# Shifting the weight tiles of 512-column products by eight offsets in turn

## The chip, the cores and the metric

The kernel runs on one core of a Trainium2 chip. The metric is the device time of one execution in microseconds (us), on the slowest core, which here is the only one. Engines are named as in the profile: PE is TensorE's matmul, PEld is TensorE's weight load, DVE is VectorE, ACT is ScalarE, POOL is GpSimd, and SP issues most of the DMAs.

## What is computed

The reference is a two-layer decoder trunk on 512 tokens of width 1024. Cut to its skeleton:

```python
for layer in range(2):
    h = rms_norm(x, ln_mix[layer])
    mem_k, mem_v = split(mem_n @ w_mem_kv[layer])            # 256 memory tokens
    if layer == 0:
        mix_out, mem_q = gated_deltanet_mixer(h, ...)         # h @ w_in, conv, chunked delta rule
    else:
        proj = h @ swa_w_q                                    # sliding-window attention, 12 heads
        mix_out, mem_q = sliding_window_attention(...), ...
    x = x + concat(mix_out, memory_attention(mem_q, mem_k, mem_v)) @ w_out[layer]
    x = x + swiglu(rms_norm(x, ln_ffn[layer]), w_gate_up[layer], w_down[layer])   # d_ff = 2816
    if layer == 0:
        shared_k, shared_v = split(rms_norm(x, ln_kv) @ w_kv)
return rms_norm(x, ln_final)
```

Everything is float32. The bulk of the arithmetic is the products of the activations with the weight matrices.

## The kernel before

Activations are kept transposed: features on the 128 partitions, the 512 tokens along the free dimension. A product of a weight tile with the activations is done in three fp32r matmuls per 128 input features: the weight and the activation are each split into a high and a low part (`whi`, `wlo` and `h`, `l`), and `mm3` issues high by high, high by low, and low by high, one after the other. In each of them the weight slice (128 partitions by 128 columns, 512 bytes per partition) is loaded into TensorE by a weight load of its own, and the activation tile is the moving operand that streams past it. The order of instructions on every engine is the order in which the code is written; PE loads the next matmul's weights while a matmul streams.

The products fall into two kinds.

- **Wide products**, 512 columns (all tokens at once), made by `project`, `row`, the loop over `down` and a few direct calls. Their weights come from `weight`, which loads a raw tile of up to 1024 columns by DMA, and splits it: ACT copies (and rounds) it into `whi`, DVE subtracts and writes `wlo` (`split`). The two tiles come from `parts`, a pool of three buffers for each name, 1088 words (of 4 bytes) a partition. By the code there are 26 wide products of 24 matmuls in the first mixer, 10 in the second, 16 for the output matrices, 8 for the first gate columns, and 16 (less two at the end) for the down projection, which takes 12 and then 10 input tiles in two weight tiles: one call of `weight` for 6 input tiles, one for the other 6 or 4. That is 624 + 240 + 384 + 192 + 528 + 468 = 2436 matmuls of 512 columns, in 120 calls of `weight`. Ten further calls of `weight` serve 252 matmuls of 256 columns (the memory's keys and values at the start, where for the values the weight tile is the moving operand, and one product at the end).
- **The ring**, 256 columns (`quarters`, 3360 matmuls): most of the gate and up columns of the feed-forward part, multiplied by a scheme that needs seven half-size products. Their weights lie in the same pool, at a fixed shift of `SHIFT` = 52 words (208 bytes) from the start of a buffer.

Where an operand lies matters here. Every buffer starts at a multiple of 256 bytes, and so do all activation tiles and all their halves; a slice of 128 columns moves a weight by 512 bytes. So in a wide product of before, the weights lie 0 bytes modulo 256 from their moving operand. In the ring the moving operand lies 48 bytes after the weights, modulo 256 (256 - 208). At the very end, the last product (tile name `T`) has weights from a pool of its own, again at 0, with 256 columns.

Of the kernel before, what the change touches and what calls it, by code (L numbers as in the profile page):

```python
# [27 lines left out]
FT = DFF // P  # L28
EPS = 1e-6
LINE = 64  # L30
SHIFT, SPARE = 52, 64
NEG = -1e30
BASE = 32
NB = P // BASE
# [54 lines left out]
class Builder:  # L89
    def __init__(self, tc, a):  # L90
        self.tc, self.nc, self.a = tc, tc.nc, a
        self.n = 0
        self.table, self.table_ins, self.table_users = None, None, []


# [97 lines left out]
    def weight(self, src, eng=None, raw=None, parts=1, pool=None, tags=("whi", "wlo"), bufs=3):  # L193

        raw = self.load(src) if raw is None else raw
        n = raw.shape[1]
        if pool is None:
            hi, lo = (x[:, :n] for x in self.parts())
        else:
            hi, lo = (self.t(pool, [P, D], F32R, t, bufs)[:, :n] for t in tags)  # L200
        for i in range(parts):
            s = slice(i * n // parts, (i + 1) * n // parts)
            self.split(raw[:, s], hi[:, s], lo[:, s], eng or self.weng)
        return hi, lo
# [1086 lines left out]
```

## Time and profile before

| | |
|---|---|
| median of 2 runs | 1148.13 us (1147.78 to 1148.49) |
| the profiled execution's own time | 1148.39 us |
| its span in the trace | 1146.6 us |
| PE / PEld busy | 98% / 86% of the span |
| DVE / ACT / POOL busy | 73% / 55% / 7% |
| granted TensorE clock | 0.998 |

Times in the trace count from the start of the span. What lies around the span is 1.8 us (1148.39 - 1146.6). A matmul's duration in the trace runs from its start to the modelled arrival of its last result, so durations of neighbours overlap; the pace of a stretch of matmuls is the time from the first start to the last, divided by their number. The view that follows the chain of work back from the last instruction, printed in order of time, gives such stretches with their length and count.

### The profile page before, as it was taken

The page shows a single profiled execution, that of the slowest core. Times are in us where ns is not written, and L with a number is a line of the kernel's source. Part 1 is how long each engine was busy: PE and PEld are TensorE (multiplying, and loading weights), DVE is VectorE, ACT ScalarE, POOL GpSimd, SP SyncE. Part 2 cuts the span into 40 slices and gives each one's busy share as a digit, 9 for nine tenths or more (in the row PEclk, how much of TensorE's full clock was granted, in tenths as well). Part 3 has the DMA queues.
Part 4 walks back from the last instruction along what each step waited for, and adds up shares of the span by engine and source line. Part 5 has one row for each costly group of instructions (what it writes and reads, how often), then busy time and mean ns, then how long its engine had stood idle before and what let it go on. Part 6 is the DMA issues. An engine that isn't in the chain of part 4 may idle for free.

```text
span 1146.6 us, 19668 instructions
## 1 busy us (share of the span) xinstructions
PE 1127.0 (98%) x7476; PEld 990.7 (86%) x7476; DVE 841.2 (73%) x1587; ACT 631.5 (55%) x1271; POOL 86.0 (7%) x97
## 2 busy tenths in 40 slices
PE   7999999999999999999999999999999999999996
PEld 5888887887899998899998777778999988999986
DVE  5764887766789987489866777759699843898754
ACT  7579572366556652256654556765566522566533
POOL 0220000000101100011100000010011100111000
PEclk9999999999999999999999999999999999999999
DMA  8333342325657744567723411144477733577232
GB/s 312 124 116 108 123 107 97 99 86 166 175 142 190 189 125 125 151 151 182 184 74 101 138 56 56 56 111 129 105 191 188 187 108 106 141 191 185 70 96 93
DMA packets 73972, 152.83 MB, mean 133 GB/s; under 512 B 17757, under 2 KB 18421, under 8 KB 73877
## 3 DMA queue, kind: packets, MB, share of 16 engines
q1 hardware_dynamic: 62356, 130.59, 36.8%
q0 software_dynamic: 11520, 20.98, 11.6%
q8 instruction: 59, 0.97, 0.4%
q14 instruction: 37, 0.30, 0.1%
HBM read 144.58 MB, written 6.96 MB: 132 GB/s over the span
## 4 chain that ended last, share of the span: by engine, by line
PE 89%; DVE 5%; ACT 4%; DMA 1%; issue 1%; SPq 0%; DVEq 0%; ACTq 0%
PE pj L154 44%; PE g L154 38%; PE sc L154 6%; ACT sm L142 2%; DVE wlo L161 1%; PE g L158 1%; DMA wraw<-in_wmk 1%; DVE q L161 0%; DVE sm L784 0%; PE qk L154 0%; ACT sm L148 0%; DVE l L164 0%; ACT whi L148 0%; ACT pf L148 0%; DVE l L161 0%
## 5 line engine op out<-in xcount | busy, mean ns | idle before, releaser
L148 ACT ACTIVATE whi<-wraw 128x512 fp32r<-128x512 f32 (+2 forms) x331 | 243.9, 746 | 244.9 <-PE pj L154 151.8
L161 DVE TENSOR_TENSOR wlo<-wraw,whi 128x512 fp32r<-128x512 f32 (+2 forms) x331 | 274.8, 840 | 102.6 <-ACT whi L148 96.8
L154 PE MATMUL pj<-h,whi 128*128 128x512 f32 (+1 forms) x676 | 267.4, 397 | 0.2 <-ACT h L148 0.2
L154 PE MATMUL pj<-l,whi 128*128 128x512 f32 (+1 forms) x676 | 264.2, 391 | 0.6 <-DVE l L164 0.4
L154 PE MATMUL pj<-h,wlo 128*128 128x512 f32 (+1 forms) x676 | 264.0, 390 | 0.0
L154 PE MATMUL g<-T,whi 128*128 128x256 f32 x1280 | 228.1, 278 | 0.2
L154 PEld LDWEIGHTS g<-T,whi 128*128 128x128 f32 x1280 | 194.7, 188 | 1.8 <-DVE fu L164 1.8
L154 PE MATMUL g<-T,wlo 128*128 128x256 f32 x640 | 177.8, 278 | 0.0
L154 PEld LDWEIGHTS pj<-h,whi 128*128 128x128 f32 x676 | 126.8, 188 | 31.2 <-issue 5.8
L154 PEld LDWEIGHTS pj<-l,whi 128*128 128x128 f32 x676 | 127.1, 188 | 26.8 <-issue 1.1
L154 PEld LDWEIGHTS pj<-h,wlo 128*128 128x128 f32 x676 | 127.0, 188 | 25.7 <-issue 0.3
L154 PE MATMUL g<-h,whi 128*128 128x256 f32 (+1 forms) x508 | 144.5, 285 | 0.0
L154 PE MATMUL g<-h,wlo 128*128 128x256 f32 (+1 forms) x508 | 144.3, 284 | 0.0
L154 PE MATMUL g<-l,whi 128*128 128x256 f32 (+1 forms) x508 | 144.2, 284 | 0.0
L154 PEld LDWEIGHTS g<-T,wlo 128*128 128x128 f32 x640 | 120.1, 188 | 0.0
L154 PEld LDWEIGHTS g<-h,whi 128*128 128x128 f32 x508 | 95.3, 188 | 1.5 <-issue 0.3
L154 PEld LDWEIGHTS g<-l,whi 128*128 128x128 f32 x508 | 95.3, 188 | 1.2
L154 PEld LDWEIGHTS g<-h,wlo 128*128 128x128 f32 x508 | 95.3, 188 | 1.1
L1025 POOL DMA_DIRECT2D ws<-in_wgu x40 | 35.4, 885 | 693.6 <-DMA ws<-in_wgu 274.9
L148 ACT ACTIVATE whi<-ws 128x512 fp32r<-128x512 f32 x80 | 50.5, 631 | 49.0 <-PE g L154 40.2
L161 DVE TENSOR_TENSOR fu<-pj,rstd 128x512 f32<-128x512 f32 (+1 forms) x34 | 22.4, 660 | 54.5 <-PE pj L154 54.4
L161 DVE TENSOR_TENSOR wlo<-ws,whi 128x512 fp32r<-128x512 f32 x80 | 54.9, 686 | 6.4 <-ACT whi L148 6.3
(355 smaller groups left out, 1617.9 us busy)
## 6 DMA issues: line engine op xcount, KB each, us to landing
wraw<-in_wgu SPq DMA_DIRECT2D x48, 512.0 KB, 4.3
ws<-in_wgu SPq DMA_DIRECT2D x80, 256.0 KB, 3.5
ws<-in_wgu POOLq DMA_DIRECT2D x80, 256.0 KB, 4.8
wraw<-in_wdn SPq DMA_DIRECT2D x48, 384.0 KB, 3.1
wraw<-in_win SPq DMA_DIRECT2D x26, 512.0 KB, 3.6
wraw<-in_wgu SPq DMA_DIRECT2D x40, 256.0 KB, 4.2
wraw<-in_wout SPq DMA_DIRECT2D x16, 512.0 KB, 3.6
wraw<-in_wdn SPq DMA_DIRECT2D x16, 256.0 KB, 2.7
```

Of the source, the lines that this page charges most:

```text
L142: ins = self.nc.scalar.activation(out, in_, func, **kw).ins
L148: self.copied = self.nc.scalar.activation(out, in_, AF.Copy, **kw).ins
L154: return self.nc.tensor.matmul(out, lhsT, rhs, start=start, stop=stop, skip_group_check=more).ins
L158: return self.nc.tensor.transpose(out, in_, self.ident[:k, :k]).ins
L161: return eng.tensor_tensor(out=out, in0=a, in1=b, op=op).ins
L1025: nc.gpsimd.dma_start(s1, a22, accum_op=ALU.add)
```

## The change

`weight` no longer puts the parts at the start of their buffers. A counter goes round a list of eight shifts, in words, and each call takes the next one for both parts. Measured from the weights up to the moving operand, modulo 256 bytes, the eight distances are 4, 252, 12, 244, 20, 236, 56 and 72 bytes. The buffers stay as large as they were; the ring and the pool of the last product are not touched.

```diff
-SHIFT, SPARE = 52, 64
+SHIFT, WIDE, SPARE = 52, (63, 1, 61, 3, 59, 5, 50, 46), 64
...
         self.n = 0
+        self.wide = 0
...
         if pool is None:
-            hi, lo = (x[:, :n] for x in self.parts())
+            o = WIDE[self.wide % len(WIDE)]
+            self.wide += 1
+            hi, lo = (x[:, o:o + n] for x in self.parts())
```

No instruction is added, removed or moved: on every engine the same instructions stand in the same order with the same waits, with other start addresses in `whi` and `wlo` (in the line numbers of helpers, one to three more). Of the 2436 wide matmuls, 318 get a distance of 4, 300 of 252, 318 of 12, 300 of 244, 312 of 20, 288 of 236, 312 of 56 and 288 of 72.

## The prediction

> **What bounds the kernel now.** I read the page's busy times first, then the chain of work that ended last, then the same chain in order of time, and last the groups of instructions by shape.
>
> ```profile
> PE 1127.0 (98%) x7476; PEld 990.7 (86%) x7476; DVE 841.2 (73%) x1587; ACT 631.5 (55%) x1271; POOL 86.0 (7%) x97
> PE 89%; DVE 5%; ACT 4%; DMA 1%; issue 1%; SPq 0%; DVEq 0%; ACTq 0%
> PE pj L154 44%; PE g L154 38%; PE sc L154 6%; ACT sm L142 2%; DVE wlo L161 1%; PE g L158 1%; DMA wraw<-in_wmk 1%; DVE q L161 0%; DVE sm L784 0%; PE qk L154 0%; ACT sm L148 0%; DVE l L164 0%; ACT whi L148 0%; ACT pf L148 0%; DVE l L161 0%
> ```
>
> The kernel is bound by PE: 89% of the chain. The wide products write banks called pj for the most part, and those alone are 44% of 1146.6 us, some 504 us; the ring writes g. So what counts is the pace at which PE takes one matmul after the other. The chain in order of time shows that pace, in stretches:
>
> ```profile
> 162.43 2.08 PE pj L154 x9
> 166.66 2.08 PE pj L154 x9
> ...
> 290.61 5.44 PE g L154 x24
> 296.05 16.32 PE pj L154 x72
> ...
> 329.60 96.60 PE g L154 x828
> 428.98 64.20 PE pj L154 x283
> 493.18 93.82 PE g L154 x805
> 592.45 46.72 PE pj L154 x206
> ...
> 679.30 2.09 PE pj L154 x9
> ...
> 1130.73 5.88 PE pj L154 x49
> ```
>
> Columns are the start, the length in us and the number of matmuls. Four paces come out of it.
>
> - Wide, in a long stretch: 16.32 / 72 = 226.7 ns a matmul of 512 columns; 64.20 / 283 = 226.9 and 46.72 / 206 = 226.8 are the same with a few slower ones at the start.
> - Wide, in the first nine matmuls after a stop: 2.08 / 9 = 231.1 ns, and 2.09 / 9 = 232.2 ns. So PE has a settled pace, and it takes some ten matmuls to reach it.
> - The ring, 256 columns at a distance of 48 bytes: 96.60 / 828 = 116.7 ns.
> - The last product, 256 columns: 5.88 / 49 = 120.0 ns, in a part where, by the addresses, the weights lie at 0 bytes.
>
> Between 120.0 (256 columns) and 226.7 (512 columns), both at 0, lie 106.7 ns for 256 columns. So 512 columns by themselves are 213.3 ns, and each matmul has some 13.3 ns beyond its columns, whatever its length; in the ring it is 116.7 - 106.7 = 10.0 ns. That remainder is all that the change can reach. The groups by shape bear the 256-column pair out, in durations that hold the pipeline too:
>
> ```profile
> L154 PE MATMUL g<-T,whi 128*128 128x256 f32 x1280 | 228.1, 278 | 0.2
> L154 PE MATMUL pj<-l,T 128*128 128x256 f32 x16 | 4.5, 283 | 0.0
> L154 PE MATMUL pj<-h,whi 128*128 128x512 f32 x660 | 262.9, 399 | 0.2 <-ACT h L148 0.2
> L154 PE MATMUL pj<-l,whi 128*128 128x512 f32 x660 | 259.7, 394 | 0.6 <-DVE l L164 0.4 <-DVE l L161 0.2
> ```
>
> 278 ns at 48 bytes against 283 at 0: the address of the weights is worth something on this chip.
>
> **The change part by part.** Nothing is added, removed or moved in any queue, so there is no term for instructions. Three things can cost or gain.
>
> *First, the settled pace at eight other distances.* The trace has no wide product at any distance but 0, so I bound it by the nearest rows. On the good side stands the ring: 120.0 - 116.7 = 3.3 ns a matmul. If all 2436 wide matmuls gained that, it would be 8.0 us; the whole remainder of 13.3 ns, which no row shows removed, would be 32.4 us. On the bad side stands the pace after a stop: 231.1 - 226.7 = 4.4 ns, 10.7 us over 2436, and 232.2 - 226.7 = 5.5 ns, 13.4 us. The two nearest rows lie at almost equal distance from today's pace. With eight distances, none of which is a multiple of 16 bytes as 48 is, some should land on each side; I take the middle of -3.3 and +4.4, which is +0.5 ns, 1.3 us. I keep -3.3 and +5.5 as ends.
>
> The Trainium skill, page "TensorE: Matmul & The Clock Gate", section "Step-by-step: what each phase is for", says that TensorE has two independent read ports into SBUF, so that loading the next weights takes nothing from the running matmul. By that rule the distance would be worth nothing, and this first term would be 0. The 278 against 283 ns, and 116.7 against 120.0, speak against it, if the two cases differ by nothing but the address; it is the ground for one of the rivals below.
>
> *Second, settling anew.* Now a whole stretch of wide products has one distance, and PE settles once: 283 matmuls at 226.9. After the change the distance is another one at each call of the weight function, after 12 to 24 matmuls. If what settles is the relation between the stream of weights and the moving stream, each call starts it afresh. A settling costs nine matmuls of 4.4 ns, 0.04 us. Of the 120 calls I take 40 to stand behind a stop already (the first mixer's scan, the attention of layer 1, where the chain has stretches of 9 matmuls as shown), a choice from the shape of the chain, which leaves 80: 80 x 0.04 = 3.2 us. Below, the bound is 0 (PE keeps its pace across the change of distance, as it does now when it goes on to another buffer); above, 120 x 0.05 = 6.0 us.
>
> *Third, the writers.* ACT writes the high part and DVE the low part at addresses that are 4, 8 or 12 bytes off a multiple of 16. Writes like that stand in the trace already, in the convolution, whose taps write from 4, 8 and 12 bytes on:
>
> ```profile
> L164 DVE SCALAR_TENSOR_TENSOR l<-x,gains,h 128x512 fp32r<-128x512 f32 x32 | 23.5, 749 | 1.5 <-ACT h L148 1.5
> L164 DVE SCALAR_TENSOR_TENSOR qv<-pj,gains,qv 128x511 f32<-128x511 f32 x11 | 8.2, 745 | 4.7 <-ACT qv L148 4.6
> L164 DVE SCALAR_TENSOR_TENSOR qv<-pj,gains,qv 128x509 f32<-128x509 f32 x11 | 8.2, 741 | 0.1
> 447.00:494.00 47.00, 47.00 (x213) 39.08 (x212) 24.33 (x37) 12.16 (x17) 4.37 (x5) 1.00 0.55 143
> ```
>
> 745 and 741 ns against 749 at an aligned address: for DVE it costs nothing. For ACT there is no such row with 512 elements. The last line is the busy time by engine over 47 us of down projection (PE, PEld, DVE, ACT, POOL): PE is busy all the time, DVE for 24.33 us and ACT for 12.16, so ACT could take half as long again and PE would still hide it. I cost the writers at 0. If that cover were gone (the scan of layer 0 and the attention, where ACT and DVE stand in the chain), one tenth more on the 4% of ACT in the chain would be some 4 to 5 us at the very most.
>
> The 252 matmuls of 256 columns that also move would gain 0.8 us at the ring's 3.3 ns, or lose as much; I leave them at 0. Of the wide matmuls' 552 us (2436 x 226.7) 504 us are in the pj part of the chain alone, so what PE gains or loses there reaches the end almost in full. A faster PE would not run into late weights in the down projection, by the same line of busy times.
>
> The sum against the profiled execution's own 1148.4 us: +1.3 for the paces, +3.2 for settling, 0 for the writers: 1152.9 us. The median of the runs shown lies 0.3 us lower than that execution, so 1152.6 us, and I put 1152.5.
>
> **The rivals.**
>
> *A gain like the ring's.* Every distance other than 0 frees the moving stream of what the ring has lost, and PE keeps its pace from product to product: -8.0 us, 1140.1 from the median. For it speaks the only measured pair of distances; against it, that this pair has 256 columns, where the weight load covers the whole matmul, and a distance of a multiple of 16 bytes, and that in a wide product half the stream runs without a weight load beside it. If the distances are better than 48, a pace of 221 ns would give -13.9 us, 1134.
>
> *PE never settles (slower).* The place is the down projection and the long stretches of 226.7 ns: there the settled pace belongs to the distance 0, and at odd distances PE stays at what it has after a stop. The price is 4.4 ns on 2436 matmuls, 10.7 us, 1158.8 us; with 5.5 ns, 1161.5 us. It decides from the point where more than half the calls do not come down to 226.7 within their 12 to 24 matmuls. For it speaks that the pace after a stop is 231 to 232 in stretches of different products; against it, that the ring, at a distance other than 0, runs at a pace just as steady, over 828 matmuls.
>
> *Nothing happens.* The difference of 3.3 ns is due to something other than the distance (the ring's matmuls write other banks), and the settled pace is kept throughout: 1148.1 us, within 1 us. That is also where the rule of two read ports would lead.
>
> **How the numbers follow.** My forecast, a mix of paces with new settling, has a chance of 0.44, and spans 1146 to 1157 us, leaving out the near-zero case. The gain has 0.31 (1132 to 1146), the unsettled PE 0.18 (1157 to 1165), nothing 0.07. A range that leaves out no more than one in ten at each end reaches to 1137 below (the gain with its better half only partly in) and to 1161 above (the unsettled pace at 4.4 ns, with a little more). Two per cent, about what a measurement of this kernel can tell from no change, is 23 us, or 9.4 ns for each wide matmul. For a gain of that size PE would have to lose almost its whole remainder, 13.3 ns down to 3.9; for such a loss it would have to run at 236 ns, more than any stretch shown. So faster by over 2% has 0.03, slower by over 2% 0.03, and within 2% 0.94.
>
> **What would show it.** In the profile of the changed kernel, the chain in order of time around the down projections has to be read for its pace: 226.9 ns over 283 matmuls becomes 228 to 229 by my forecast, 223 by the gain, 231 by the unsettled PE. Since the distances go in turn, the starts of the matmuls inside one product show the pace of that distance: I expect some of the eight under 226.7 and some over, and the first ten of a product slower than the rest. The group of 660 matmuls named pj<-l,whi should go from 394 ns to 395 to 397; DVE's and ACT's splits should keep their durations; the ring should stay at 116.7 and the last product's T matmuls at 283 ns. I am wrong if a product at one distance shows no slow start (no settling), or if all eight distances lie on one side of 226.7.

## The result, and the profile after

The changed kernel takes 1157.82 us (median of 2 runs, 1157.55 to 1158.1) against 1148.13: a ratio of 1.0085, 95% interval 1.006 to 1.0109. It is slower by 9.7 us: inside the wide range of 1137 to 1161 us and within 2%, but more than twice the loss of the forecast (4.4 us), and just outside the 1146 to 1157 us that belonged to the forecast's own mechanism. The span of the profiled execution went from 1146.6 to 1156.3 us at the same granted clock, 0.998.

The page's busy times and its chain by engine:

```profile
span 1156.3 us, 19668 instructions
PE 1137.0 (98%) x7476; PEld 991.0 (86%) x7476; DVE 840.4 (73%) x1587; ACT 631.5 (55%) x1271; POOL 86.0 (7%) x97
PE 90%; DVE 4%; ACT 3%; DMA 1%; issue 1%; SPq 0%; DVEq 0%; ACTq 0%
```

The number of instructions is the same, the writers (DVE, ACT) and the weight loads (PEld) are as busy as before, and PE is busy for 10.0 us more. The chain in order of time (start, length, number of matmuls; lines left out are marked) tells where:

```profile
298.33 16.76 PE pj L155 x72
...
332.71 96.60 PE g L155 x828
432.11 65.78 PE pj L155 x283
...
597.16 47.78 PE pj L155 x206
...
925.05 65.77 PE pj L155 x283
...
1140.47 5.85 PE pj L155 x49
```

The stretch of 72 wide matmuls, 226.7 ns each before, is at 16.76 / 72 = 232.8; the 283 of each down projection went from 226.9 to 232.4 ns, the 206 from 226.8 to 231.9. The ring, in g, stands at 96.60 / 828 = 116.7 ns as it did. So the loss sits in the pace of the wide products, all over the program.

For the pace at each distance I took the starts of successive wide matmuls from the trace, and the distance of each from the built program's addresses (stops, gaps of 260 ns and more, left out). The mean is 232.2 ns, 227.5 before, a difference of 4.7. Of the 2436 wide matmuls 2242 follow another one in this way; 4.7 x 2242 = 10.5 us, which is near the 10.0 us that PE is busier and the 9.7 us of the kernel. By distance, from the tenth matmul of a product on (a product here is a run of matmuls into one bank at one distance):

| distance, bytes | 4 | 252 | 12 | 244 | 20 | 236 | 56 | 72 | 0 (before) |
|---|---|---|---|---|---|---|---|---|---|
| mean pace, ns | 232.9 | 232.5 | 233.0 | 232.9 | 231.6 | 233.3 | 230.6 | 231.9 | 226.7 |

All eight means lie on the bad side. None shows a slow start and a fall: at 236 bytes the first matmuls take 232.3, 230.9, 232.2, 233.1, and then it is 233.3 to the end. The starts fall into short patterns that repeat, such as 231 229 232 235 at 20 bytes.

One correction to the description above: the buffers do not start at multiples of 256 bytes but 192 bytes above one, weights and activations alike. The distances are as stated.

### The profile page after: what moved, and what is told of

It is laid out like the page before. It is cut to its first block, busy times and chain, and to the rows that moved or that the text cites. A ratio compares the mean times of both kernels' runs of the same rounds, so it can differ in the third digit from the quotient of the medians.

```text
span 1156.3 us, 19668 instructions
## 1 busy us (share of the span) xinstructions
PE 1137.0 (98%) x7476; PEld 991.0 (86%) x7476; DVE 840.4 (73%) x1587; ACT 631.5 (55%) x1271; POOL 86.0 (7%) x97
## 4 chain that ended last, share of the span: by engine, by line
PE 90%; DVE 4%; ACT 3%; DMA 1%; issue 1%; SPq 0%; DVEq 0%; ACTq 0%
PE pj L155 45%; PE g L155 38%; PE sc L155 6%; ACT sm L143 2%; DVE wlo L162 1%; PE g L159 1%; DMA wraw<-in_wmk 1%; DVE q L162 0%; DVE sm L787 0%; DVE l L165 0%; PE qk L155 0%; ACT sm L149 0%; DMA kn<-q 0%; ACT whi L149 0%; ACT pf L149 0%
```

## The experiments

Eleven kernels were run. All but one differ from the changed kernel in the list of shifts alone (a shift of s words is a distance of 256 - 4 s bytes).

**One distance or eight.** Is it the distances, or going from one to the next at each call?

```diff
-SHIFT, WIDE, SPARE = 52, (63, 1, 61, 3, 59, 5, 50, 46), 64
+SHIFT, WIDE, SPARE = 52, (61,), 64        # distance 12
+SHIFT, WIDE, SPARE = 52, (52,), 64        # distance 48, the other kernel
```

> All wide products at one distance, 12 bytes, instead of eight in turn. Theory A (each distance has a settled pace of its own; what the changed kernel showed at 12 bytes was 233.3 ns from the second half of a product on): every long stretch of wide products settles at 233.3 ns, the down projections' stretch of 283 matmuls takes 66.0 us, and the time is 1148.1 + 2436 x (233.3 - 226.7) x 0.85 = some 1161 to 1163 us, slower than the eight in turn. Theory B (a distance as such costs nothing, but changing it from call to call keeps PE from settling): 226.7 ns, and 1148 to 1150 us.

> All wide products at the ring's distance, 48 bytes. Theory A with a gain like the ring's (3.3 ns a matmul): a pace of 223.4 ns, and 1140 us. Theory A, if what helps 256 columns does not help 512 (a matmul stream of twice the length, with a weight load beside half of it only): a pace between 228 and 232 ns, 1151 to 1158 us. Theory B: 226.7 ns and 1148 us. The prediction's first term rested on the first of these.

Distance 12 took 1159.62 us (ratio 1.0098, 1.0082 to 1.0113), 48 took 1156.36 us (1.0073, 1.0056 to 1.009), against 1148.01 of the kernel before, run beside them. The chain of distance 12, then of 48:

```profile
432.39 66.02 PE pj L155 x283
```

```profile
430.52 65.62 PE pj L155 x283
```

66.02 / 283 = 233.3 ns at 12 bytes and 65.62 / 283 = 231.9 at 48. The pace at 12 is that of theory A, the time a little under its 1161 to 1163 us. So a single distance, kept throughout, is as slow as eight in turn: going from one to the next is not what costs. And the ring's distance, which beside 256 columns leaves 10.0 ns beyond the columns, leaves 231.9 - 213.3 = 18.6 ns beside 512. The gain of the ring does not carry over; it changes sign.

**Which distances are good.** Three lists of eight, one run each:

```diff
+... WIDE ... (60, 56, 52, 48, 44, 40, 36, 32)     # 16, 32, ... 128
+... WIDE ... (28, 24, 20, 16, 12, 8, 4, 0)        # 144, 160, ... 240, 0
+... WIDE ... (62, 58, 54, 42, 38, 34, 30, 26)     # 8, 24, 40, 88, ... 152
```

> The eight distances 16, 32, 48, 64, 80, 96, 112 and 128 bytes in turn, so that one profile shows the pace of each. Theory A: each has its own pace; multiples of 64 may behave as 0 does (226.7), the others 228 to 233; time 1150 to 1158 us. Theory C (only distances that are no multiple of 16 cost, since their weights begin inside a line of 16 bytes): all eight run at 226.7 or less, 1140 to 1149 us. Theory B: all slow, 231 to 233, since they change from call to call.

> The eight distances 144, 160, 176, 192, 208, 224, 240 and 256 (that is, 0) bytes in turn. Theory A: the products at 0 run at 226.7 ns among the others, the rest at 228 to 233, and the paces mirror those of 112 down to 16 if only the size of the distance counts; 1150 to 1157 us. Theory C: all at 226.7 or less. Theory B: the products at 0 are as slow as the rest, 231 or more.

> The eight distances 8, 24, 40, 88, 104, 120, 136 and 152 bytes in turn, to see whether any beats the 226.7 ns of 0. Theory A with a narrow best place from 0 to 16 bytes: 8 between 226.7 and 230, 24 near 228 to 231, the others 230 to 234; 1155 to 1158 us. If the good place is only at exact multiples of 16 next to 0: 8 and 24 at 231 to 233 as well.

They took 1155.14, 1157.41 and 1156.53 us. The pace from the tenth matmul on, in ns, worked out as above:

| | | | | | | | |
|---|---|---|---|---|---|---|---|
| 16: 227.6 | 32: 233.4 | 48: 231.8 | 64: 228.6 | 80: 230.0 | 96: 233.6 | 112: 233.2 | 128: 233.1 |
| 144: 233.3 | 160: 234.1 | 176: 231.9 | 192: 233.4 | 208: 233.4 | 224: 233.3 | 240: 233.4 | 0: 226.7 |
| 8: 233.3 | 24: 231.2 | 40: 232.3 | 88: 233.3 | 104: 231.3 | 120: 233.3 | 136: 226.7 | 152: 233.3 |

Theory C (only weights off a line of 16 bytes are slow) falls: 32, 96, 144 and 160 are as slow as any, and 48 was slow alone. It is no mirror image either (16 is good, 240 is not), and no narrow place around 0 (8 is bad, 136 is good). The products at 0 stand at 226.7 among seven bad ones, which they reach in some ten matmuls (232, 232, 230, 230, 229, 228, 228, 227, 228, 227). That is the settling of the prediction: the first ten average some 229.1, about 24 ns a call beyond 226.7. These are paces in turn; what that can hide shows below.

**The good distances in turn, and alone.**

```diff
+... WIDE ... (0, 60)      # 0 and 16
+... WIDE ... (60,)        # 16
```

> Only the two good distances, 0 and 16 bytes, in turn from call to call. It separates the two terms of the prediction: the paces of both are known (226.7 settled at 0, 227.5 at 16), so what is beyond them is the cost of settling anew. Theory A with settling (at 0 among seven other distances the first ten matmuls averaged 229.2 ns, 26 ns a call beyond the settled pace): 1148.0 + 1218 x 0.9 ns + some 80 to 120 calls x 26 ns = 1151.1 to 1152.2 us. Without settling: 1149.1 us. If a change of distance keeps PE from ever settling: 1158 us.

> All wide products at the one distance of 16 bytes. Theory A: settled pace of 227.5 ns over the whole of the long stretches, 1148.0 + 2436 x 0.9 ns = 1149 to 1150.5 us, and 1 to 3 us less than 0 and 16 in turn. If 16 settles at exactly what 0 has when it is left alone: 1148 us.

0 and 16 in turn: 1147.76 us, ratio 1.0 (0.999 to 1.0009). 16 alone: 1148.31 us, ratio 1.0004 (0.9995 to 1.0014). Both are no change. The 3 to 4 us that I expected for settling anew did not come: going from 0 to 16 keeps the pace. So a change of distance need not cost anything of itself; the new settling at 0 was seen behind products at a bad pace, and behind stops.

Nor is 16 bytes a distance with one pace of 227.5 ns, as theory A had it. The chain of 16 alone has two:

```profile
427.44 64.15 PE pj L155 x283
...
590.86 47.05 PE pj L155 x206
```

64.15 / 283 = 226.7 ns and 47.05 / 206 = 228.4 (228.3 once settled): two paces at the same distance in the same kernel, each kept over a whole stretch. The 227.6 of the table is a mean of the two.

**The weights' address, the moving operand's, or the distance.** In one kernel the activations of one pool were shifted too, and calls alternated between shifts of 0 and 12 bytes (the three smaller buffer counts that made room are not shown here):

```diff
+SHIFT, WIDE, SPARE = 52, (0, 3), 64
...
+        if pool is getattr(self, "bpool", None):
+            return tuple(self.t(pool, [P, T + 64], F32R, tag + p, bufs)[:, 3:3 + T] for p in "hl")
```

> Weights of wide products in turn at shifts of 0 and 12 bytes, and the activation tiles of one of the two pools shifted by 12 bytes as well, the other pool's not. So there are four combinations: both unshifted (distance 0), both shifted by 12 (distance 0), only the moving operand shifted (distance 12), only the weights shifted (distance 244). Three buffer counts elsewhere are one smaller to make room. Theory A (it is the distance between weights and moving operand): the two combinations at distance 0 settle at 226.7 ns alike, the other two at 232.5 to 233.5. Theory D (it is the weights' own address, off a line or off what the writers and the weight load like): weights at 0 settle at 226.7 whatever the moving operand's shift, weights at 12 are slow even at distance 0. The total says little, since the ring's distances move with the activations.

1150.86 us in one run. Long products settled at 226.7 ns with both unshifted, as expected. With both shifted, again a distance of 0, it was 228.9, and with only the moving operand shifted (distance 12) 228.9 too, where distance 12 by shifted weights had given 233.3. So neither theory holds as it stands. All six long products with both shifted stayed at 228.9, one of them straight behind a stop, which speaks for the moving operand's own address counting beside the distance; that they merely kept a state, as found next, is not ruled out by this one run. And there was a surprise in its first down projection, whose activations were not shifted: calls at 0 and at 244 alternated, and both ran at 226.7 (64.16 / 283), though 244 had been among the slowest.

```profile
429.88 64.16 PE pj L155 x283
...
1133.36 5.76 PE pj L155 x49
```

The second line is the last product, of 256 columns, most of whose matmuls lie at a distance of 12 bytes in this kernel: 5.76 / 49 = 117.6 ns, against 120.0 at 0 in the kernel before. So the addresses seem to move the pace of 256 columns as well, with the same output banks as before.

**The same distance at several paces.** The 244 bytes at 226.7 ns led to a new theory, E: a distance can have more than one settled pace, and where a product begins decides which. The test is the same list without the shifted activations, and 244 bytes alone:

```diff
+... WIDE ... (0, 3)       # 0 and 244
+... WIDE ... (3,)         # 244
```

> Distances of 0 and 244 bytes in turn, nothing else changed. With eight distances in turn, products at 244 ran at 233.3 or 230.4 ns for the most part; with shifted activations, where calls at 0 and 244 alternate, those of the first down projection ran at 226.7. Theory E (a distance has more than one settled pace, and which of them PE takes is decided by the state in which the product begins: behind a product settled at 0 it stays at 226.7): products at 244 behind one at 0 without a stop run at 226.7 in the long stretches, and the time is 1148 to 1151 us. Theory A (the pace belongs to the distance alone): products at 244 run at 231 to 233, 1148 + 1218 x 5 ns = 1153 to 1156 us.

> All wide products at the one distance of 244 bytes. Theory E: with no product at 0 to lead into the good state, PE settles after each stop where it happens to land, at 226.7 in some stretches, and at 230.4 or 233.3 in others, with one pace kept over a whole stretch of products without a stop; 1152 to 1160 us, slower than 0 and 244 in turn by 3 us or more although half of the products are the same. Theory A: 231 to 233 everywhere, 1158 to 1161 us, and 0 and 244 in turn lies half way.

0 and 244 in turn: 1148.17 us, ratio 1.0007 (0.9997 to 1.0016), no change. 244 alone: 1156.23 us, ratio 1.0076 (1.0062 to 1.009). Theory A wanted the first half way between 0 and 244 alone; it isn't. Chains in order of time, first of 0 and 244 in turn, then of 244 alone:

```profile
428.64 64.20 PE pj L155 x283
...
917.75 64.16 PE pj L155 x283
```

```profile
113.06 16.56 PE pj L155 x72
...
430.00 66.03 PE pj L155 x283
...
789.79 16.79 PE pj L155 x72
...
923.63 65.08 PE pj L155 x283
```

In turn, the down projections run at 226.9 and 226.7 ns, though half their weights lie at 244. The whole trace of that kernel has 40 products at 244 with 16 matmuls or more. The 29 that follow at least two matmuls at 0 without a stop all settle at 226.7 ns. Of the 11 that open a stretch, or have one matmul at 0 ahead of them, 6 settle at 230.0, 4 at 233.3 and 1 at 226.7. So at the same distance, in one kernel, the pace goes by what ran just before. Alone, the same work at the same distance runs at 66.03 / 283 = 233.3 ns in layer 0 and at 65.08 / 283 = 230.0 in layer 1; the stretches of 72 at 230.0 and 233.2. The starts of single matmuls, in the timeline of that kernel, show two different rhythms (start, duration):

```profile
940.03 0.39 PE L155 MATMUL pj<-h,wlo 128*128 128x512 f32 x1
940.25 0.40 PE L155 MATMUL pj<-h,whi 128*128 128x512 f32 x1
940.49 0.39 PE L155 MATMUL pj<-l,whi 128*128 128x512 f32 x1
940.71 0.40 PE L155 MATMUL pj<-h,wlo 128*128 128x512 f32 x1
```

```profile
470.21 0.39 PE L155 MATMUL pj<-ac11l,whi 128*128 128x512 f32 x1
470.44 0.39 PE L155 MATMUL pj<-ac11h,wlo 128*128 128x512 f32 x1
470.67 0.39 PE L155 MATMUL pj<-h,whi 128*128 128x512 f32 x1
```

In layer 1 starts lie 0.22 and 0.24 us apart by turns (224 and 236 ns in the trace's own resolution), in layer 0 always 0.23 (233.3). In that kernel the pattern changed only behind a stop or an interlude of other matmuls, and then lasted over all products to the next. Theory E fits all of it but one detail: it had expected some stretches of 244 alone at 226.7, and none is there. What in the hardware holds the state was not tried.

**A distance that settles faster.** 136 bytes had settled after three matmuls.

```diff
+... WIDE ... (30,)        # 136
```

> All wide products at the one distance of 136 bytes, the only one of the 31 tried beside 0 and 16 at which products in turn settled at 226.7 ns, and there after three matmuls, not ten. If it comes down as fast after a stop: the long stretches stay at 226.7 and each of some 60 to 100 starts saves some 15 to 25 ns against the distance 0, so 1146 to 1147.5 us, 1 to 2 us under the kernel before. If the fast settling was owed to what ran ahead of it: 1148 us or a little more.

1146.96 us against 1147.45, ratio 0.9998 (0.9989 to 1.0007): not to be told from the kernel before. The pace does what was expected, a mean of 227.0 ns against 227.5, settled after three matmuls (231.8, 229.8, 227.6, 226.9), which is some 1.1 us of PE; the measured time doesn't show it. No distance tried beats 0 by more than that.

## Why the prediction was right, and where it was not

*The bound* was read rightly: PE's pace, with the down projections and gate columns as its place. The loss is PE's pace times the number of wide matmuls that follow each other; 10.5 us of matmuls made 9.7 us of time. That loss also stands clear of no change (ratio 1.006 at the least), so a measurement of this kernel tells far less than two per cent from no change.

*The first term, the settled pace,* is where the size went wrong. I took the middle of -3.3 and +4.4 ns, +0.5; the eight distances measured +4.7 on the mean of all matmuls. Both ends came from rows, but the good end was no neighbour of the wide products: at the ring's own distance 512 columns ran at 231.9 ns, 5.2 slower than at 0. The bad end, the pace after a stop (231.1 to 232.2), was the nearer neighbour in size. That most distances leave PE in just that condition is a reading which no run tested; the steady 233.3 ns lies beyond it. So the term should have been some +10.5 us, not +1.3.

*The second term, settling anew,* was 3.2 us in the sum. In the changed kernel it does not appear, since PE comes down to 226.7 at almost no product there. With 0 and 16 in turn it is 0 within the interval. Where it exists (0 among seven bad ones) it is about 24 ns a call, against the 40 I took. The sum had the smaller term too large and the larger one far too small.

*The third term, the writers,* was 0 and is: DVE's splits of 512 elements from `wraw` took 690 ns before and 689 after, ACT's 628 and 628:

```profile
L162 DVE TENSOR_TENSOR wlo<-wraw,whi 128x512 fp32r<-128x512 f32 x217 | 146.2, 689 | 34.0 <-ACT whi L149 28.6
L149 ACT ACTIVATE whi<-wraw 128x512 fp32r<-128x512 f32 x217 | 133.8, 628 | 89.0 <-PE pj L155 43.4 <-PE g L155 37.9 <-ACT h L149 2.9
```

*The rivals.* What happened is nearest to the one I gave 0.18, PE that never settles, with its price of 10.7 us (10.5 in matmuls, 9.7 in time) and its place. Its word "never settles" needs mending: PE does settle, in a steady pattern, at 230 to 233 ns. I had held against it that the ring's pace is steady; steady it was here too, and slow. The gain like the ring's is refuted by the run at 48 bytes. One ground I gave for doubting it was misread, though: that half the stream of a wide product runs without a weight load beside it. The line of busy times in the prediction has PEld busy for 39.08 of 47.00 us. "Nothing" is refuted by distance 12 alone, 233.3 ns against 226.7; and the last product at 117.6 ns above speaks against its ground, that the 3.3 ns between ring and last product were not due to the addresses. I had drawn "the distance is worth nothing" from the rule of two independent read ports (the Trainium skill, "TensorE: Matmul & The Clock Gate", "Step-by-step: what each phase is for"). That conclusion fails on the 233.3 against 226.7 ns; whether the ports are independent, no run here shows. The two signs I named for being wrong, no slow start and all eight on one side, both came. The forecast's own mechanism, some distances good and some bad with a settling at each call, was wrong: that the time fell into the range was luck, owed to a range wide enough to hold the rival.

*The controls* held: the ring at 116.7 ns (96.60 / 828 above), and the last product's matmuls at 283:

```profile
L155 PE MATMUL pj<-l,T 128*128 128x256 f32 x16 | 4.5, 283 | 0.0
```

## What to carry to other kernels

Where PE is the bound and its matmuls follow each other without a gap, read the pace of long stretches (length over count in the chain) and compare it with the columns; a few ns per matmul can hang on the addresses of the two operands. A gain from placing weights at one width need not carry over to another (48 bytes: 3.3 ns better at 256 columns, 5.2 worse at 512): measure the width itself, one candidate per product in turn, and read each from the starts in one trace. But such a screening shows each candidate in the state its neighbours leave, so run the candidate alone as well before believing it: 244 bytes looked like 0 beside it, and cost 0.8% alone.

## What was not expected of the hardware

- The address of the weights moves the pace of a 512-column fp32r matmul between 226.7 and 234.1 ns. Of 32 distances tried in turn, 0 and 136 settled at 226.7, 16 had a mean within a nanosecond of it, 64 within two.
- At one and the same distance several steady paces are possible: at 244 bytes 230.0 and 233.3 ns alone, and 226.7 behind products at 0; at 16 bytes alone 226.7 and 228.3. Each was kept over stretches of 200 and more matmuls. At 12 bytes alone it was 233.3, and 226.7 in two short products near the start.
- Several steady paces are whole multiples of one time: 226.7 and 233.3 ns are 34 and 35 times 6.67 ns, 120.0 is 18 times, the pair of 224 and 236 is 69 times. That reads like a beat of 6.67 ns into which the matmuls fall. It is only a reading: the 231.9 ns at 48 bytes fits no such simple multiple, and what would beat was not tried.
